# Rotary tables of three supertiles in one set, and the sums of one group's second V weights declared a step later

## The chip, the cores and the metric

The kernel runs on one core of a Trainium2 chip. The metric is the device time of one execution in microseconds; of several runs the median is taken.

## What is computed

A two-layer encoder over 2048 tokens of width 1024. In each layer a normed row is projected to eight sections; four feed a softmax attention over the token's own chunk of 64 and the eight before it (8 heads of 64, a learned bias by distance), four feed a retention (4 heads of 128) whose queries and keys are turned by rotary phases. Both outputs are gated, put side by side and projected back onto the row.

```
def rotary_tables(positions, dim):
    ang = positions.astype(jnp.float32)[:, None] * inv_freq[None, :]
    return jnp.cos(ang), jnp.sin(ang)
...
    hn = rms_norm(x, norm_gain)
    proj = hn @ w_in.astype(hn.dtype)
    aq, ak, av, ag, rq, rk, rv, rg = jnp.split(proj, cuts, axis=-1)
    ya = chunked_rel_attention(aq, ak, av, rel_bias)
    yr = chunkwise_retention(rq, rk, rv, cos, sin)
    y = jnp.concatenate([ya * jax.nn.silu(ag), yr * jax.nn.silu(rg)], axis=-1)
    return x + y @ w_out.astype(x.dtype)
```

## The kernel before

The tokens are cut into 4 supertiles `n` of 512 (16 token tiles of 128), the heads of a layer into 4 groups `s`. For each group and supertile two dense products are made, `dense_T` (tiles `dT`, line 778: q and k of both parts, tokens along the columns) and `dense_V` (tiles `dV`, line 797: v, the retention's v and the gates), each of four 512-wide tiles of 24 matmuls; operands are split in a high and a low half (`hTh`, `hTl` for the rows, `whT`, `wlT`, `whV`, `wlV` for the weights), three products for each pair. In between stand the attention and retention of the supertile before.

`run()` sets the order. In each round it advances the dense generator by eight matmuls, ticks the list of postponed steps (`later(k, ...)` runs a step k rounds on), takes one step of the attention, and draws steps from a background list `bg`: as many as the declared steps still to come, divided by the rounds left, rounded up. The engines' order is the program's order; only the queue of SyncE (SP), which issues nearly all DMAs, is ordered by the scheduler after the start. Sums and retention products share four small PSUM buffers in rotation, the dense tiles two.

Four pieces matter here. `tables(ns, wk)` works out cosine and sine for the supertiles `ns` in four workspaces: DMAs of the positions (line 90), an angle on ScalarE (100), a reduction of 15 steps on VectorE (lines 94, 97, 98, 107, 114, 116), sine activations on ScalarE behind a load of their function table (118, 119, 121), and stores to DRAM (127 to 130). Workspaces are 256 columns wide for each supertile, on 128 partitions. `norms_from_input(ts, ...)` norms the token tiles `ts` of the first layer: load of x (line 1239), square on ScalarE (212), root on GpSimd (POOL, 219), scaling on VectorE (1251), high and low half (234, 238), and two DMA transposes (243, 244) into `hTh`, `hTl`. `prep_V(l, s, g)` quantizes the next group's V weights in four sections: load (305), square with its sum along the row (320), a cast (327), a sum over partitions by a one-column matmul `msV` (334), a scale (336 and 151 to 155), and the two halves (341 on ScalarE, 344 on VectorE). `rest(k)` in it lets k background steps pass between a square and its sum. The attention's softmax is at lines 845 to 857 (scores, scale and maximum, exponential, product with the bias on POOL, transpose `pT`), its output at 865 to 877, the retention's products `r` at 899, the rotary turn on POOL at 719 to 721, and the evacuations of the dense tiles at 677 to 697 (`qq`, `kk`) and 805 to 815 (`v`, `rv`, `gt`).

The first group's start is an order written out by hand, in which `u` is a step of the table generator `t1` for supertiles 1 and 2. The tables of supertile 3 ride in the second `norms_from_input`, a step per round, on two halves of the same buffers.

Of the kernel before, what the change touches and what calls it, by code (L numbers as in the profile page):

```python
# [10 lines left out]
F32 = mybir.dt.float32  # L11
# [7 lines left out]
P = 128  # L19
# [8 lines left out]
def hybrid_trunk(ctx: ExitStack, tc: tile.TileContext, x, pos, gain, gcol, w_in, w_out, rel, fgain,  # L28
                 invf, dmask, dcol, out):
    nc = tc.nc  # L30
    SEQ, D = x.shape
# [14 lines left out]
    w4 = ctx.enter_context(tc.tile_pool(name="w4", bufs=3))  # L46
# [36 lines left out]
    def tables(ns, wk):  # L83

        ang, k, r, k2 = wk
        pi = k2.bitcast(I32)
        for i, n in enumerate(ns):
            for hf in range(2):
                o = n * 512 + hf * 256
                sp.dma_start(pi[hf * 64:(hf + 1) * 64, i * 256:(i + 1) * 256], pos[None, o:o + 256].to_broadcast([64, 256]))  # L90
        yield

        def mulsub(dst, kk, c):
            dve.scalar_tensor_tensor(out=dst, in0=kk, scalar=-c, in1=dst, op0=ALU.mult, op1=ALU.add)

        def rnd(dst, src, mul):
            dve.tensor_scalar(dst, src, mul, MAGIC, op0=ALU.mult, op1=ALU.add)
            dve.tensor_scalar(dst, dst, -MAGIC, None, op0=ALU.add)

        act.activation(ang, pi, AF.Copy, scale=invf_sb[:, 0:1])  # L100
        yield
        rnd(k, ang, 1.0 / P1)
        yield
        for c in (PA, PB, PC):
            mulsub(ang, k, c)
            yield
        dve.scalar_tensor_tensor(out=k2, in0=k, scalar=-(PD + PE_), in1=ang, op0=ALU.mult, op1=ALU.add)
        yield
        rnd(k2, k2, 1.0 / TWO_PI)
        yield  # L110
        for kk, c in ((k2, QA), (k, PD), (k2, QB), (k, PE_), (k2, QC)):
            mulsub(ang, kk, c)
            yield
        dve.tensor_scalar(ang, ang, PI_CL, -PI_CL, op0=ALU.min, op1=ALU.max)
        yield
        dve.scalar_tensor_tensor(out=k, in0=ang, scalar=-1.0, in1=ang, op0=ALU.mult, op1=ALU.max)
        yield
        act.activation(r, ang, AF.Sin)
        act.activation(k2, k, AF.Sin, scale=-1.0, bias=quarter[:, 0:1])
        yield  # L120
        act.activation(ang, r, AF.Copy, scale=-1.0)
        yield
        def store(i, n, hf):
            sl = slice(hf * 64, hf * 64 + 64)
            cs = slice(hf * 256, hf * 256 + 256)
            ws = slice(i * 256, i * 256 + 256)
            sp.dma_start(tab_d[n][0, 0:64, cs], k2[sl, ws])
            sp.dma_start(tab_d[n][0, 64:128, cs], k2[sl, ws])
            sp.dma_start(tab_d[n][1, 0:64, cs], ang[sl, ws])
            sp.dma_start(tab_d[n][1, 64:128, cs], r[sl, ws])  # L130
            if hf == 1:
                tab_done.add(n)

        for hf in range(2):
            store(0, ns[0], hf)
            if len(ns) > 1:
                later(7 + 4 * hf, lambda hf=hf: store(1, ns[1], hf))
        yield

    TAB_STEPS = 18  # L140
# [301 lines left out]
    def prep_V(l, s, g):  # L442
        nm = f"V{l}_{s}"
        g.vh = b3.tile([P, KT, 512], F16, tag="wh", name=f"wh{nm}")
        g.vl = b3.tile([P, KT, 512], F16, tag="wl", name=f"wl{nm}")
        c0 = s * P
        sts = []

        def ld(j):
            o = VSEC[j] * 512 + c0  # L450
            sts.append(load_sec(w_in[l, :, o:o + P], f"{nm}{j}"))

        def sq(j):
            return sumsq(sts[j], f"{nm}{j}", g.vh[:, :, j * P:(j + 1) * P])

        def cv(j, s_):
            return convert(sts[j], g.vh[:, :, j * P:(j + 1) * P], g.vl[:, :, j * P:(j + 1) * P], s_)

        def rest(k):
            for _ in range(k):  # L460
                yield

        ld(0)
        ld(1)
        yield
        iv = [None] * 3
        m1 = [None] * 2
        for j in range(2):
            yield
            m1[j] = lowp(sq(j), f"{nm}{j}")  # L470
            yield from rest(3)
            m = allsum(m1[j], f"{nm}{j}")
            sv, iv[j] = norm_scale(m, f"{nm}{j}", gains[l].i)
            yield from cv(j, sv)
            ld(2 + j)
        yield from rest(1)
        m2 = sq(2)
        yield
        yield from rest(1)
        m3 = sq(3)  # L480
        dve.tensor_tensor(m2, m2, m3, op=ALU.add)
        m2 = lowp(m2, f"{nm}2")
        yield
        yield from rest(2)
        m = allsum(m2, f"{nm}2")
        sv, iv[2] = norm_scale(m, f"{nm}2", gains[l].i)
        for _ in V_units(l, s, g, iv, nm):
            pass
        yield from cv(2, sv)
        yield from cv(3, sv)  # L490
        g.vdone = 4
# [145 lines left out]
    def later(k, fn):  # L637
        deferred.append([k, fn])
# [556 lines left out]
    def push(gen, steps):  # L1195
        bg.append([gen, steps])
# [17 lines left out]
    def grp(l, s):  # L1214
        if (l, s) not in groups:
            groups[l, s] = Grp()
        return groups[l, s]
# [12 lines left out]
                pull(min(-(-todo // max(left, 1)), todo))  # L1230
            left -= 1

    def norms_from_input(ts, spaces, rows, tab):

        def load(k):
            u = us[k]
            u.x = spaces[k] if spaces else w4.tile([P, D], F32, tag="w4", name=f"xin{u.t}")
            if not spaces:
                sp.dma_start(u.x, x[u.t * P:(u.t + 1) * P, :])

        def sq(k):
            u = us[k]
            u.h = [h_[:, :, u.t % 4 * P:(u.t % 4 + 1) * P] for h_ in hT_of(0, u.t // 4)]
            u.ss = squares(u.x.rearrange("p (k c) -> p k c", c=P), u.nm, u.h[0])

        def root(k):
            us[k].rs = rms_of(us[k].ss, gains[0].m, gains[0].e, us[k].nm)

        def mul(k):
            u = us[k]  # L1250
            dve.scalar_tensor_tensor(out=u.x, in0=u.x, scalar=u.rs[:, 0:1], in1=gains[0].b, op0=ALU.mult, op1=ALU.mult)

        def hi(k):
            us[k].rows = rows[k % 2]
            rows_hi(us[k].rows, us[k].x)

        def lo(k):
            rows_lo(us[k].rows, us[k].x)

        def dma(k):  # L1260
            transpose_rows(us[k].rows, *us[k].h)

        us = []
        for t in ts:
            u = St()
            u.t, u.nm = t, f"n0_{t}"
            us.append(u)
        plan = {0: [lambda: load(0)]}
        add = lambda r, fn, k: plan.setdefault(r, []).append(lambda: fn(k))
        for k in range(4):  # L1270
            if k:
                add(4 * k - 4, load, k)
            for i, fn in enumerate((sq, root, mul, hi, lo, dma)):
                add(3 + 4 * k + i, fn, k)
        for r in range(21):
            for fn in plan.get(r, ()):
                fn()
            next(tab, None)
            yield
        for _ in tab:  # L1280
            yield

    xa = b3.tile([P, 2, D], F32, tag="wh", name="xa")
    xb = b3.tile([P, 2, D], F32, tag="wl", name="xb")
    xs0 = [xa[:, 0, :], xa[:, 1, :], xb[:, 0, :], xb[:, 1, :]]
# [48 lines left out]
    late = [h_.rearrange("p k c -> p (k c)").bitcast(F32)[:, i * D:(i + 1) * D] for f in far for h_ in f for i in range(2)]  # L1334
# [70 lines left out]
            vu.append(V_units(0, 0, g00, scs["V0"].i + scs["V2"].i, "V0_0"))  # L1405
        next(vu[0])

    t1 = tables((1, 2), [xs0[1 + i // 2][:, i % 2 * 512:(i % 2 + 1) * 512] for i in range(4)])
    x8 = (sp.dma_start(late[t - 8], x[t * P:(t + 1) * P, :]) for t in range(8, 12))
    steps = {"x8": lambda: go_on(x8), "d": lambda: go_on(d0), "t": lambda: go_on(t0), "u": lambda: go_on(t1), "r": lambda: go_on(rl_), "g": lambda: go_on(gs),  # L1410
             "Tu": T_un, "Vu": V_un, "bs": lambda: go_on(bs0), "bt": lambda: go_on(bt0)}
# [26 lines left out]
    for l in range(DEPTH):  # L1438
        gO = [Grp(), Grp()]
        go = Grp()  # L1440
        for s in range(NSW):
            g = grp(l, s)
            for n in range(NS):
                first = (l, s, n) == (0, 0, 0)
# [11 lines left out]
                if (l, s) == (0, 0) and 0 < n < NS - 1:  # L1456
                    if n == 1:
                        push(t1, TAB_STEPS - 7)
                    pairs = [xs0[0], w4.tile([P, D], F32, tag="w4", name="rows8") if n == 1 else xs0[1]]
                    pairs = [(w_[:, 0:D], w_[:, D:2 * D]) for w_ in (r_.bitcast(F16) for r_ in pairs)]  # L1460
                    push(norms_from_input(range(4 * n + 4, 4 * n + 8), late[0:4] if n == 1 else None, pairs,
                                          iter(()) if n == 1 else tables((3,), [xs0[3][:, i * 256:(i + 1) * 256] for i in range(4)])), 21)
                if (l, s, n) == (0, 1, 1):
                    for l_ in range(1, DEPTH):
                        gr = gain_scale(l_)
# [17 lines left out]
                    run(dT, att, 12 if last else 10 if n == 0 else 18 if (l, s, n) == (0, 0, NS - 1) else 22 if (l, s) == (0, 0) else 24)  # L1483
                if n == NS - 1:
                    if s + 1 < NSW:
                        push(prep_V(l, s + 1, grp(l, s + 1)), 23)
                    else:
                        push(with_turn(prep_O(l, 1, gO[1], go), us), 12)
                run(dense_V(l, s, n, g, st), att, 24 if n == NS - 1 and s < NSW - 1 else 12)
# [90 lines left out]
```

## Time and profile before

| | |
|---|---|
| runs | 2061.4, 2063.08, 2059.04 us; median 2061.4 |
| profiled execution | 2062.49 us, span 2060.7 us |
| mean granted clock of TensorE | 0.995 |
| busy, share of span | PE 97%, VectorE 60%, ScalarE 55%, POOL 33% |

The span is the time from the first to the last instruction in the profiled execution. PE is TensorE's matmuls, PEld its weight loads, DVE VectorE, ACT ScalarE, POOL GpSimd, SP SyncE. A row of the timeline gives start (us), duration (us), engine, line, operation, what it writes and reads, and in brackets how long the engine stood idle before it and what released it. Rows grouped by line give the busy time in all, the mean in ns, and the idle time before.

### The profile page before, as it was taken

Reading aid. Unit: us, or ns where it says so; the run is one execution under the profiler, and the core shown is the slowest. Engines: PE = TensorE matmul, PEld = TensorE weight load, DVE = VectorE, ACT = ScalarE, POOL = GpSimd, SP = SyncE. Lnnn points to the kernel's source line nnn. Section 1 sums busy time; section 2 is a strip of 40 time slices with the busy share of each in tenths; the row PEclk is TensorE's granted clock in tenths of the full one; section 3 lists DMA queues with packets and bytes.
Section 4 is the critical chain, followed back from the end, with each engine's and each line's share of the span. In section 5 each row is a group of like instructions: output and inputs, shape, how many; then the busy total and the mean of one; then the engine's idle time right before and its main releaser. Section 6 shows DMA issues by size and latency. Waiting matters only on the chain. (4 is left out here: it accounts for less than half of the span.)

```text
span 2060.7 us, 39339 instructions
## 1 busy us (share of the span) xinstructions
PE 1999.4 (97%) x14038; PEld 1052.9 (51%) x14038; DVE 1228.1 (60%) x3804; ACT 1134.8 (55%) x2526; POOL 688.1 (33%) x701
## 2 busy tenths in 40 slices
PE   6988999999999999999999999999999999999998
PEld 4444555555555555554444555555555555555544
DVE  6776666565556555666553556555655566557643
ACT  6556665556565645555444546655656565455432
POOL 0344343434334434430003443444333334333100
PEclk9999999999999999999999999999999999999999
DMA  8778664547584754899774546554746775658864
GB/s 227 169 161 178 155 148 109 112 114 164 117 185 113 165 128 101 174 209 263 219 185 113 124 104 156 116 126 103 158 117 150 148 155 124 129 115 187 224 203 139
DMA packets 645701, 313.64 MB, mean 152 GB/s; under 512 B 459232, under 2 KB 602080, under 8 KB 645504
## 3 DMA queue, kind: packets, MB, share of 16 engines
q1 hardware_dynamic: 645504, 311.12, 65.6%
q8 instruction: 110, 1.80, 0.4%
q14 instruction: 87, 0.71, 0.1%
HBM read 123.26 MB, written 41.98 MB: 80 GB/s over the span
## 5 line engine op out<-in xcount | busy, mean ns | idle before, releaser
L855 POOL TENSOR_TENSOR pq<-sc,pq 128x640 f16<-128x640 f32 (+4 forms) x256 | 319.4, 1248 | 860.5 <-ACT pq L854 443.8
L852 ACT ACTIVATE sc<-sc,mq,cT 128x640 f32<-128x640 f32 (+4 forms) x256 | 218.4, 853 | 615.6 <-DVE rl L871 309.7
L797 PE MATMUL dV<-whV,hTh 128*128 128x512 f16 x1024 | 353.9, 381 | 7.3 <-DVE gt L815 6.1
L797 PE MATMUL dV<-whV,hTl 128*128 128x512 f16 x1024 | 353.8, 381 | 0.0
L797 PE MATMUL dV<-wlV,hTh 128*128 128x512 f16 x1024 | 353.8, 381 | 0.0
L778 PE MATMUL dT<-hTh,whT 128*128 128x512 f16 x1008 | 346.6, 379 | 2.7 <-DVE kk L697 1.3
L778 PE MATMUL dT<-hTl,whT 128*128 128x512 f16 x1008 | 346.6, 379 | 0.0
L778 PE MATMUL dT<-hTh,wlT 128*128 128x512 f16 x1008 | 346.6, 379 | 0.0
L797 PEld LDWEIGHTS <-hTh 128*128 128x128 f16 x2048 | 197.0, 98 | 224.7 <-DVE gt L815 10.0
L778 PEld LDWEIGHTS <-whT 128*128 128x128 f16 x2016 | 192.1, 98 | 207.7 <-issue 1.6
L849 DVE CUSTOM_DVE_ANT_0 sc<-S,bias 128x640 f32<-128x640 f32 (+4 forms) x256 | 188.3, 735 | 88.8 <-PE S L846 87.4
L1172 PE MATMUL dO<-whO,yly 128*128 128x512 f16 x504 | 191.0, 379 | 1.7 <-DMA yly<-hTl 1.1
L1172 PE MATMUL dO<-whO,yhy 128*128 128x512 f16 x504 | 191.0, 379 | 1.0 <-DMA yhy<-hTh 1.0
L1172 PE MATMUL dO<-wlO,yhy 128*128 128x512 f16 x504 | 191.0, 379 | 0.0
L854 ACT ACTIVATE pq<-sc 128x640 f16<-128x640 f32 (+4 forms) x256 | 171.5, 670 | 8.1
L797 PEld LDWEIGHTS <-hTl 128*128 128x128 f16 x1024 | 99.4, 98 | 112.4 <-issue 3.9
L1172 PEld LDWEIGHTS <-yhy 128*128 128x128 f16 x1008 | 98.1, 98 | 113.7 <-DMA yhy<-hTh 1.5
L778 PEld LDWEIGHTS <-wlT 128*128 128x128 f16 x1008 | 97.2, 98 | 113.7 <-issue 6.0
L845 PE MATMUL S<-k,q 128*128 128x128 f16 (+3 forms) x592 | 142.4, 267 | 0.0
L865 PE MATMUL o<-v,pT 128*128 128x65 f16 x1120 | 129.8, 193 | 6.4 <-DMA pT<-pq 5.5
L866 PE MATMUL o<-v,pT 128*128 128x64 f16 x1120 | 130.1, 195 | 0.0
L846 PE MATMUL S<-k,q 128*128 128x128 f16 (+3 forms) x592 | 129.7, 267 | 0.0
(359 smaller groups left out, 3476.5 us busy)
## 6 DMA issues: line engine op xcount, KB each, us to landing
q<-qq SPq DMA_DIRECT2D x128, 128.0 KB, 2.4
yyy<-y_d SPq DMA_DIRECT2D x32, 512.0 KB, 4.5
stT<-in_w_in_dram SPq DMA_DIRECT2D x27, 512.0 KB, 4.8
stV<-in_w_in_dram SPq DMA_DIRECT2D x26, 512.0 KB, 4.6
k<-kk SPq DMA_DIRECT2D x128, 64.0 KB, 2.0
swp<-rot SPq DMA_DIRECT2D x64, 128.0 KB, 3.1
tabc<-tab SPq DMA_DIRECT2D x32, 256.0 KB, 3.0
tabs<-tab SPq DMA_DIRECT2D x32, 256.0 KB, 3.1
```

The source lines that it names most:

```text
L778: pe.matmul(ps, w_[:, j, kt, :], h_[:, kt, :], start=(m == 0), stop=(m == 23))
L797: pe.matmul(ps, h_[:, kt, a * P:(a + 1) * P], w_[:, kt, :], start=(m == 0), stop=(m == 23))
L845: pe.matmul(o, st.q[:, hx, 0, cs], k_, start=True, stop=False)
L846: pe.matmul(o, st.q[:, hx, 1, cs], k_, start=False, stop=True)
L849: dve.tensor_tensor_reduce(out=v, in0=S[:, 0:w], in1=g.bias[hx][:, 640 - w:640], scale=1.0, scalar=-3.0e38, op0=ALU.add, op1=ALU.max, accu ...
L852: act.activation(v, v, AF.Exp, bias=m[:, 0:1], scale=g.c[:, 0:1])
L854: act.activation(pq[:, 0:w], v, AF.Copy)
L855: pool.tensor_tensor(pq[:, w:2 * w], v, pq[:, 0:w], op=ALU.subtract)
L865: pe.matmul(o[:, 0:65], u.p[:, b, :], v_[:, 0:65], start=(b == 0), stop=False)
L866: pe.matmul(o[:, 0:64], u.p[:, b, :], v_[:, 65:129], start=False, stop=False)
L1172: pe.matmul(ps, h_[:, kt, :], w_[:, kt, :], start=(m == 0), stop=(m == 23))
```

## The change

The tables of supertiles 1, 2 and 3 are worked out together, 768 columns wide, by the generator that made those of 1 and 2; a further buffer `wkc` serves as fourth workspace. `norms_from_input` loses its tables. The stores of the two later supertiles are postponed by 3, 6, 9 and 12 rounds instead of 7 and 11 for one. For the second group of the first layer, `prep_V` rests a step more between the first, second and last square and their sums, and its declared number of steps is 26 instead of 23.

```diff
-            if len(ns) > 1:
-                later(7 + 4 * hf, lambda hf=hf: store(1, ns[1], hf))
+            for i in range(1, len(ns)):
+                later(6 * i - 3 + 3 * hf, lambda i=i, hf=hf: store(i, ns[i], hf))
...
+        first = (l, s) == (0, 1)
...
-            yield from rest(3)
+            yield from rest(3 + first)
...
-        yield from rest(2)
+        yield from rest(2 + first)
...
-    def norms_from_input(ts, spaces, rows, tab):
+    def norms_from_input(ts, spaces, rows):
...
-            next(tab, None)
-            yield
-        for _ in tab:
             yield
...
-    t1 = tables((1, 2), [xs0[1 + i // 2][:, i % 2 * 512:(i % 2 + 1) * 512] for i in range(4)])
+    wk = [xb.rearrange("p a c -> p (a c)")[:, 0:768], xs0[1][:, 0:768], xb.rearrange("p a c -> p (a c)")[:, 768:1536],
+          w4.tile([P, D], F32, tag="w4", name="wkc")[:, 0:768]]
+    t1 = tables((1, 2, 3), wk)
...
-                                          iter(()) if n == 1 else tables((3,), [xs0[3][:, i * 256:(i + 1) * 256] for i in range(4)])), 21)
+                    push(norms_from_input(range(4 * n + 4, 4 * n + 8), late[0:4] if n == 1 else None, pairs), 21)
...
-                        push(prep_V(l, s + 1, grp(l, s + 1)), 23)
+                        push(prep_V(l, s + 1, grp(l, s + 1)), 26 if (l, s) == (0, 0) else 23)
```

How instructions move is seen in the order of each engine. (From line 463 on, the changed file counts one line more, up to the end of `norms_from_input`.) On ScalarE, at the end of the second `norms_from_input`, before:

```order
L854 ACTIVATE pq_0_1_2_1_2142<-sc_0_1_2_1_2137 128x640
L212 ACTIVATE hTh_3_150,ssn_15_2147<-xin_1903 128x8x128
L118 ACT_TABLE_LOAD
L118 ACTIVATE xb<-xb 128x256
L119 ACTIVATE xb<-xb,quarter 128x256
L730 ACTIVATE rot_0_2_2_1889<-rot_0_2_2_1889 128x512
L947 ACTIVATE state_0_0_1229<-state_0_0_1229 128x128
L121 ACTIVATE xb<-xb 128x256
L805 ACTIVATE v_0_2_2000<-dV_0_2_1_2102 128x2x64
L806 ACT_TABLE_LOAD
L806 ACTIVATE gt_0_2_1_2185<-dV_0_2_1_2102,ughV_0_735 128x256
L807 ACTIVATE rv_0_2_1_2184<-dV_0_2_1_2102,urvV_0_733 128x128
```

And after, at the same place:

```order
L855 ACTIVATE pq_0_1_2_1_2135<-sc_0_1_2_1_2130 128x640
L212 ACTIVATE hTh_3_150,ssn_15_2140<-xin_1903 128x8x128
L731 ACTIVATE rot_0_2_2_1889<-rot_0_2_2_1889 128x512
L948 ACTIVATE state_0_0_1236<-state_0_0_1236 128x128
L806 ACTIVATE v_0_2_1996<-dV_0_2_1_2095 128x2x64
L807 ACTIVATE gt_0_2_1_2175<-dV_0_2_1_2095,ughV_0_738 128x256
L808 ACTIVATE rv_0_2_1_2174<-dV_0_2_1_2095,urvV_0_736 128x128
```

The three table activations and two loads of function tables are gone from between token tile 15's square (`ssn_15`) and the evacuation of a dense tile. (In the names of the dense tiles the first number is the group, the second the supertile.)

On TensorE, at the first sum of the second group's V weights (`msV_10`) in the dense tile `dV_0_3_2`, whose first third stands ahead of the attention step that ends with `r_0_11`. Before:

```order
L899 LDWEIGHTS rot_0_2_3_1980
L899 MATMUL r_0_11_3064<-rot_0_2_2_1889,rot_0_2_3_1980 128x128
L334 LDWEIGHTS ones
L334 MATMUL msV_10_3069<-mbV_10_2971,ones 128x1
L797 LDWEIGHTS hTh_3_150
L797 MATMUL dV_0_3_2_3022<-wlV_0_199,hTh_3_150 128x512
L797 LDWEIGHTS hTh_3_150
L797 MATMUL dV_0_3_2_3022<-whV_0_198,hTh_3_150 128x512
```

After, where `dV_0_3_2` begins:

```order
L900 MATMUL r_0_10_2992<-rv_0_2_2_2272,kt_0_2_2361 128x128
L334 LDWEIGHTS ones
L334 MATMUL msV_10_3004<-mbV_10_2953,ones 128x1
L798 LDWEIGHTS hTh_3_150
L798 MATMUL dV_0_3_2_3016<-whV_0_198,hTh_3_150 128x512
L798 LDWEIGHTS hTl_3_151
L798 MATMUL dV_0_3_2_3016<-whV_0_198,hTl_3_151 128x512
```

The sum has moved ahead of the tile's first eight matmuls and of the attention step behind them. The square that feeds it has kept its place on ScalarE; before:

```order
L852 ACTIVATE sc_0_2_2_1_2960<-sc_0_2_2_1_2960,mq_0_2_2_1_2961,cT_0_676 128x640
L854 ACTIVATE pq_0_2_2_1_2965<-sc_0_2_2_1_2960 128x640
L320 ACTIVATE whV_1_2919,m1V_10_2969<-stV_10_2921 128x8x128
L730 ACTIVATE rot_0_3_2_2678<-rot_0_3_2_2678 128x512
L947 ACTIVATE state_0_0_1229<-state_0_0_1229 128x128
```

After:

```order
L853 ACTIVATE sc_0_2_2_1_2942<-sc_0_2_2_1_2942,mq_0_2_2_1_2943,cT_0_679 128x640
L855 ACTIVATE pq_0_2_2_1_2947<-sc_0_2_2_1_2942 128x640
L320 ACTIVATE whV_1_2901,m1V_10_2951<-stV_10_2903 128x8x128
L731 ACTIVATE rot_0_3_2_2660<-rot_0_3_2_2660 128x512
L948 ACTIVATE state_0_0_1236<-state_0_0_1236 128x128
```

The second sum (`msV_11`) moves in the same way, ahead of the first eight matmuls of `dT_1_0_0`; its square moves ahead of one softmax step. The third sum keeps its place on TensorE, and one of its two squares moves ahead of a softmax step.

More of the change, by code (lines that the diff above doesn't have):

```diff
@@ L1460, in hybrid_trunk @@
                     pairs = [(w_[:, 0:D], w_[:, D:2 * D]) for w_ in (r_.bitcast(F16) for r_ in pairs)]
-                    push(norms_from_input(range(4 * n + 4, 4 * n + 8), late[0:4] if n == 1 else None, pairs,
-                                          iter(()) if n == 1 else tables((3,), [xs0[3][:, i * 256:(i + 1) * 256] for i in range(4)])), 21)
+                    push(norms_from_input(range(4 * n + 4, 4 * n + 8), late[0:4] if n == 1 else None, pairs), 21)
                 if (l, s, n) == (0, 1, 1):
```

## The prediction

> **What bounds the kernel now.** I read the page first, then the waits of TensorE, then cuts of the 3.41 us that its clock moves in, and last the timeline at the three places that the change touches. The page says which engine sets the time:
>
> ```profile
> span 2060.7 us, 39339 instructions
> PE 1999.4 (97%) x14038; PEld 1052.9 (51%) x14038; DVE 1228.1 (60%) x3804; ACT 1134.8 (55%) x2526; POOL 688.1 (33%) x701
> ```
>
> TensorE (PE) works for 97% of the span. The change takes no matmul away, so it can gain or lose only where PE stands still or runs slow. Between 60 and 300 us, which holds all that is edited, the waits of PE are these (us in total, times, longest):
>
> ```profile
> PE dV L797 <- DVE gt L815: 4.9, 2, 3.3
> ...
> PE msV L334 <- DVE ya L877: 3.4, 3, 1.5
> ...
> PE dT L778 <- DVE kk L697: 1.3, 1, 1.3
> ...
> PE dT L778 <- DMA hTh<-xa: 0.8, 1, 0.8
> PE dT L778 <- DVE qq L680: 0.6, 1, 0.6
> ```
>
> The first row holds the stall beside the tables of supertile 3, the second the sums of the V weights, the third and the fifth stand in the tables of supertiles 1 and 2. The second price of a stall is the clock. In cuts of 3.41 us, each row gives the stretch, PE's busy time, and behind POOL's the granted clock:
>
> ```profile
> 90.32:93.73 3.41, 2.23 (x14) 1.16 (x14) 1.96 (x8) 1.81 (x3) 0.00 (x0) 1.00 0.44 104
> 117.62:121.03 3.41, 0.78 (x6) 0.28 (x5) 3.41 (x4) 2.81 (x11) 3.33 (x3) 1.00 0.61 125
> 121.03:124.44 3.41, 3.24 (x13) 1.64 (x14) 2.99 (x10) 0.65 (x1) 1.94 (x3) 0.50 0.98 305
> 179.05:182.47 3.42, 1.21 (x6) 0.36 (x4) 0.00 (x0) 3.40 (x8) 2.82 (x3) 1.00 0.83 204
> 182.47:185.88 3.41, 2.36 (x6) 0.89 (x7) 3.26 (x9) 0.39 (x2) 0.00 (x0) 0.50 0.67 187
> 185.88:189.30 3.42, 3.42 (x26) 2.08 (x25) 1.38 (x5) 3.33 (x6) 1.40 (x1) 0.50 0.43 153
> ```
>
> A stretch with 0.78 or 1.21 us of work is followed by one at half clock; a stretch with 2.23 is not. A stretch at half clock and 2.36 us busy is followed by a second. So I price a wait of over some 2.2 us within one stretch at 3.41 / 2 = 1.7 us more, if PE is what is late just after. Whether a wait falls into one stretch or over two is chance.
>
> **A, tables of 768 columns (70 to 91.5 us).** Sizes and slack:
>
> ```profile
> L116 DVE SCALAR_TENSOR_TENSOR xa<-xa 128x512 f32<-128x512 f32 x1 | 0.7, 693 | 0.0
> ...
> L116 DVE SCALAR_TENSOR_TENSOR xb<-xb 128x256 f32<-128x256 f32 x1 | 0.4, 419 | 0.0
> L114 DVE TENSOR_SCALAR xa<-xa 128x512 f32<-128x512 f32 x1 | 0.4, 417 | 0.0
> ...
> L114 DVE TENSOR_SCALAR xb<-xb 128x256 f32<-128x256 f32 x1 | 0.3, 285 | 0.0
> ```
>
> ```profile
> L119 ACT ACTIVATE xb<-xa,quarter 128x512 f32<-128x512 f32 x1 | 0.7, 705 | 0.0
> ...
> L119 ACT ACTIVATE xb<-xb,quarter 128x256 f32<-128x256 f32 x1 | 0.5, 492 | 0.0
> ```
>
> ```profile
> 74.16 0.29 DVE L811 SCALAR_TENSOR_TENSOR v<-dV,v 128x128 f16<-128x128 f32 x1 [0.64 <-ACT rv L807]
> ...
> 82.41 0.69 DVE L727 TENSOR_TENSOR rot<-raw,rot 128x512 f16<-128x512 f32 x1 [0.64 <-POOL pq L855]
> ...
> 83.82 0.69 DVE L680 SCALAR_TENSOR_TENSOR qq<-dT,qq 128x512 f16<-128x512 f32 x1 [0.71 <-ACT qq L677]
> ...
> 87.18 1.28 ACT L118 ACT_TABLE_LOAD   x1
> ...
> 91.50 0.38 PE L778 MATMUL dT<-hTh,whT 128*128 128x512 f16 x1 [1.28 <-DVE kk L697]
> ```
>
> Another 256 columns cost 0.27 us in a SCALAR_TENSOR_TENSOR, 0.13 in a TENSOR_SCALAR, 0.21 on ScalarE (ACT). Ahead of the table load at 87.18 DVE has nine steps of the first kind and four of the second: 9 x 0.27 + 4 x 0.13 = 3.0 us more, against slack of 0.64 + 0.64 + 0.71 = 2.0. So the softmax step ahead of that load, and the load, come 1.0 later; the three ACTIVATEs behind it add 3 x 0.21 = 0.64; kk L694 and L697 stand behind them in order, and PE at 91.50 behind L697. That is **+1.6**, between 0.6 (only the ACTIVATEs count) and 2.6 (1.0 of the slack isn't there, since POOL's work beside stretches some of these steps). The waits of 0.6 and 1.3 become some 1.0 and 2.5 us. That is enough for a half clock where it falls into one stretch: 0.6 x 1.7 = **+1.0**.
>
> Here the Trainium skill speaks against me: "TensorE: Matmul & The Clock Gate", section "HAM oscillation — how this bites in real kernels", has as its rule no idle gaps over about 3.4 us, so that this wait would cost its own length alone and the sum would be 1.0 lower. The stretch at 121.03 disagrees: it runs at 0.50 behind one that had 0.78 us of work, not none.
>
> **D, the queue of SyncE (118 to 133 us).** The eight stores for two supertiles instead of four for one now stand among these transfers, and the two first loads of x for supertile 3 come right ahead of the transposes of token tile 11. The transpose that now stands right behind the loads, the second of tile 11, which stands clear of them, and PE's first use of tile 11:
>
> ```profile
> L243 SPq DMA_TRANSPOSE hTh<-xa x1: 2434/2434/2434, 121.9 to 121.9; - x1
> ...
> DMA to landing us min/median/max: 5.2/5.2/5.2
> ```
>
> ```profile
> L244 SPq DMA_TRANSPOSE hTl<-rows x1: 1231/1231/1231, 129.8 to 129.8; - x1
> ...
> DMA to landing us min/median/max: 3.0/3.0/3.0
> ```
>
> ```profile
> 133.02 1.46 PE L778 MATMUL dT<-hTh,whT 128*128 128x512 f16 x6
> ```
>
> The second half of tile 11 is issued at 129.8 and lands at 132.8; PE needs it in its third matmul, 133.4 (six matmuls in 1.46 us start 0.22 apart). With 5.2 it would land at 135.0. The loads have been under way some 4 us by then, so I take the middle: **+0.7**, between 0 and 1.5. The loads of positions move too, to the queue near 45 us, where the next transposes wait for ACT anyway: 0.
>
> **B, tables of supertile 3 gone (158 to 194 us).** Fifteen DVE steps, four ACTIVATEs and two table loads leave, and eight stores behind them.
>
> ```profile
> 173.51 0.23 PE L899 MATMUL r<-rv,dT 128*128 128x128 f16 x1 [1.29 <-DVE dT L907]
> ...
> 181.40 0.55 POOL L219 TENSOR_TENSOR rsn<-ssn,mhalf 128x1 f32<-128x1 f32 x1
> ...
> 183.38 1.28 DVE L1251 SCALAR_TENSOR_TENSOR xin<-xin,rsn,gb 128x1024 f32<-128x1024 f32 x1
> ...
> 183.52 0.61 PE L797 MATMUL dV<-whV,hTh 128*128 128x512 f16 x1 [3.26 <-DVE gt L815]
> ...
> 193.93 1.25 PE L778 MATMUL dT<-hTh,whT 128*128 128x512 f16 x5 [0.77 <-DMA hTh<-xa]
> ```
>
> The waits at 173.51 and 183.52 lose their cause. But what is late next is the norm of token tile 15: POOL takes its root (181.40) behind the rotary turn, DVE scales the row (183.38), then softmax, the high half, POOL, SyncE's transpose, and PE at 193.93. POOL keeps its work and its order; it comes 1.29 earlier with PE. The scaling then starts at 181.40 + 0.55 - 1.29 = 180.7 instead of 183.38, and with the same chain behind it PE is released **-2.7** us at 193.93. The ends are -1.4 (POOL no earlier) and -4.8, by this row:
>
> ```profile
> L94 DVE SCALAR_TENSOR_TENSOR xb<-xb 128x256 f32<-128x256 f32 x8 | 6.7, 843 | 0.0
> ```
>
> Eight steps of the tables take 843 ns instead of the 419 of the row above, beside POOL; if all of these 8 x 0.42 = 3.4 us came to POOL's chain, it would be -1.4 - 3.4. PE is then early for the new release at 191.2: from 183.52 to 193.93 it takes 10.41 - 0.77 - 2.89 (half of 2.36 + 3.42, at half clock) = 6.75 us, and it starts at 183.52 - 3.26 - 1.29 = 178.97, so it idles 191.2 - 185.7 = 5.5 us in several pieces; for the stretch behind the start that is 0.5 x 1.7 = **+0.8**.
>
> **C, the sums of the second V weights (234 to 268 us).** By the order in the section on the change, the first sum comes a round earlier, not later: the total of declared steps rises, and two steps are drawn per round for longer. Its square stays where it is.
>
> ```profile
> 234.69 0.38 PE L797 MATMUL dV<-whV,hTh 128*128 128x512 f16 x1
> ...
> 237.02 1.04 ACT L320 ACTIVATE whV<-stV 128x1024 f16<-128x1024 f32 x1
> ...
> 238.19 0.16 DVE L327 CAST mbV<-m1V 128x1 bf16<-128x1 f32 x1 [2.79 <-ACT whV L320]
> ...
> 238.98 0.16 PE L334 MATMUL msV<-mbV,ones 128*128 128x1 bf16 x1 [1.22 <-DVE ya L877]
> ```
>
> PE reaches the sum at 234.69 and must hold it until the cast has ended, 238.40: 3.7 us, with a third of a dense tile and an attention step queued behind that could have run. Their work, 238.98 - 1.22 - 234.69 = 3.07, follows: they end at 241.47 instead of 239.01, +2.4. The other two waits of the row of 3.4 go, as their squares come earlier: -(3.4 - 1.2) = -2.2. Together **+0.2**, between -1.5 (casts earlier than now, by slack that I don't see) and +1.5 (the third wait stays). A single wait of 3.7 nearly always empties one stretch: 0.9 x 1.7 = **+1.5**.
>
> **Sum.** 1.6 + 1.0 + 0.7 - 2.7 + 0.8 + 0.2 + 1.5 = +3.1 on the profiled execution's 2062.49. That one stands 1.1 above the median of the runs, 2061.4; so 2064.5.
>
> **Rivals.** *Each wait earns its half clock, and C two stretches,* as at 182.47 to 189.30: 1.6 + 1.7 + 0.7 - 2.7 + 1.7 + 0.2 + 3.4 = +6.6, 2068.0, slower. For it: every wait over 2.2 us within one stretch that the rows show. Against: none is sure to fall so. It decides once two of the three do. Chance 0.25.
> *The norm of tile 15 doesn't bind:* then 1.29 + 3.26 + 0.77 of waits and 2.89 of half clock go, -8.2 in place of -1.9, and the sum is -3.2: 2058.2, or 2057 if A keeps its clock. For it: the wait at 193.93 is only 0.77 long. Against: the scaling can't start before POOL's root. Chance 0.13.
> *No half clock for waits under 3.4 us,* by the mechanism that a stretch must be empty: without 1.0 and 0.8 the sum is +1.3, 2062.7. The row at 121.03 speaks against it. This is the page's rule above. Chance 0.07.
> *The edit does what its words say,* each sum behind its square: 1.6 + 1.0 + 0.7 - 1.9 - 3.4 = -2.0, 2059.4. Only if the printed order weren't what runs. Chance 0.05. My forecast has 0.5.
>
> About 0.2%, 4.1 us, is what a measurement of this kernel can tell from no change. Slower by more (over 2065.5): 0.22 of the first rival and 0.21 of the forecast, whose own 8 in 10 are 2061 to 2068: 0.43. Faster (under 2057.3): half of the second rival, some of the fourth and the tail: 0.15. Within: 0.42. The range from 2058.0 to 2069.5 takes in the first rival and the second in part.
>
> **What would show it.** In the profile after: kk L697 releases PE 1.3 to 2 us later against the first tables' start, with a wait of about 2.5; the waits for gt L815 lose the one of 3.3 us, and dT L778 waits for hTh of tile 15 for longer than 0.8; msV L334 waits once, some 3.7 us, for its own cast, with a half-clock stretch behind it. I am wrong if PE no longer waits at supertile 3's start, if msV's first wait is short, or if the clock stays at 1.00 behind waits of 2.5 us.

## The result and the profile after

The change makes the kernel slower: 2068.05 us against 2062.02 us (medians of 21 runs each), a ratio of 1.0028 with a 95% interval of 1.0021 to 1.0034, or 4.3 to 7.0 us. The profiled execution after takes 2068.73 us with a span of 2066.5.

The waits of TensorE between 60 and 300 us, after (us in total, times, longest):

```profile
PE msV L334 <- DVE mbV L327: 3.5, 1, 3.5
PE o L866 <- DMA pT<-pq: 2.8, 3, 1.1
...
PE dT L779 <- DVE kk L698: 2.2, 1, 2.2
PE dT L779 <- DMA hTh<-rows: 1.2, 1, 1.2
PE dT L779 <- DVE qq L681: 1.2, 1, 1.2
PE dT L779 <- DMA hTh<-xa: 0.8, 1, 0.8
```

The 4.9 us behind gt L815 are gone, and so are the three waits of a sum for an evacuation. (Of the 4.9, 3.3 stood beside the tables of supertile 3. The other 1.6 stood near 68 us, ahead of the steps that change; this execution is 1.6 us late there, by a stretch at half clock from 44.86 us, and that wait takes it up.) In their place stand one wait of 3.5 us of the first sum for its own cast, longer waits in the first tables (kk and qq, and 1.0 us in two for rot), and waits for DMA transposes (pT, hTh<-rows). The granted clock in cuts of 3.41 us (the column behind POOL's) around the wait for sh L908, which before has too, behind supertile 3's start, and around the first sum:

```profile
119.96:123.37 3.41, 1.10 (x15) 0.48 (x12) 3.04 (x2) 3.38 (x12) 3.41 (x3) 1.00 0.70 136
123.37:126.78 3.41, 2.69 (x12) 1.33 (x12) 2.98 (x11) 0.26 (x1) 2.69 (x4) 0.50 0.46 109
126.78:130.20 3.42, 3.42 (x10) 1.22 (x9) 2.81 (x8) 3.11 (x5) 1.16 (x1) 0.50 0.70 148
...
191.64:195.05 3.41, 1.32 (x10) 0.52 (x9) 3.41 (x10) 1.73 (x8) 0.55 (x2) 1.00 0.64 138
195.05:198.46 3.41, 2.59 (x9) 1.02 (x10) 1.38 (x6) 2.45 (x6) 0.71 (x1) 0.50 0.81 162
198.46:201.88 3.42, 3.42 (x25) 1.97 (x24) 1.08 (x4) 0.51 (x2) 0.68 (x1) 0.50 1.50 241
...
239.42:242.84 3.42, 0.40 (x4) 0.28 (x5) 1.06 (x4) 2.26 (x3) 0.53 (x1) 1.00 0.62 173
242.84:246.25 3.41, 2.73 (x8) 1.04 (x8) 2.01 (x12) 2.33 (x9) 3.33 (x4) 0.50 0.43 99
246.25:249.66 3.41, 3.41 (x36) 2.02 (x34) 2.16 (x6) 1.75 (x2) 1.27 (x1) 1.00 0.06 17
```

Each stretch at full clock with 1.32 us of work or less is followed by one at half clock, as before. A halved stretch with 2.59 or 2.69 us of work had a second behind it, one with 2.73 had none.

Where the time went, by the start of the same matmul in both traces: PE is 3.2 us late when kk releases it (94.66 against 91.50), 5.8 late at the first matmul of supertile 2 (138.83 against 133.02), 2.5 at the first of supertile 3 (196.43 against 193.93). The two halved stretches behind that take most of this gain back: just ahead of the first sum PE is 5.1 late (239.57 against 234.46). It is 8.8 late behind the first sum (243.54 against 234.69), and 6.2 behind the third (273.90 against 267.68); it ends 5.8 later. So in this execution the tables' part makes 5.1 us and the sums some 1.1.

### The profile page after: what moved, and what is told of

It reads as the page before. It is cut to its first block, busy times and chain, and to the rows that moved or that the text cites. A ratio compares the mean times of both kernels' runs of the same rounds, so it can differ in the third digit from the quotient of the medians.

```text
span 2066.5 us, 39310 instructions
## 1 busy us (share of the span) xinstructions
PE 2002.7 (97%) x14038; PEld 1052.8 (51%) x14038; DVE 1222.8 (59%) x3789; ACT 1133.0 (55%) x2520; POOL 686.1 (33%) x701
```

## The experiments

Each is compared with before in runs on one chip, 9 to 11 runs of it against 21 to 33 of before; a ratio of 1.0010 is 2.1 us.

**The two parts alone.** The tables' part has the whole diff but that of `prep_V` and its declared steps; the sums' part has only these.

> The tables' part of the change alone. From the two traces, theory 1 says that this part carries the loss: PE comes to 91.5 of before some 3.2 us late (first tables wider and SyncE's queue longer ahead of them), loses some 3 us more to transposes that land late around 120 to 148, and gets back about 3 us and two half-clock stretches where the tables of supertile 3 were, of which a later half clock takes most: about +4.5 us against before (+3 to +6). Theory 2, that the loss is the sum which PE holds for 3.5 us, says that the tables alone are within 1.5 us of before.

> The V sums' part alone (rests one step longer, 26 declared steps). Theory 1: one wait of 3.5 us and about one half-clock stretch come, waits of 1.2, 0.7 and 1.5 us go: +1 us against before (-0.5 to +2.5). Theory 2, that this wait and the clock behind it carry the loss: +3.5 to +5 us.

The tables alone: 1.0017 (1.0008 to 1.0026), +3.5 us. The sums alone: 1.0013 (1.0004 to 1.0022), +2.7 us. The sum of the two, 6.2, is about the whole change's 5.8: the loss is shared. Theory 2 falls for the tables, which cost more than the 1.5 us it gave them. Theory 1's range holds the tables; the sums lie 0.2 above its range, but their own interval (0.8 to 4.5) reaches into it. The profile of the sums alone shows how they can cost more than its +1: PE is 0.3 late ahead of the first sum and 2.8 behind the third, with this clock:

```profile
234.08:237.49 3.41, 0.74 (x10) 0.45 (x9) 1.62 (x7) 1.69 (x3) 0.00 (x0) 1.00 0.55 150
237.49:240.91 3.42, 2.17 (x7) 0.80 (x7) 1.55 (x8) 2.81 (x8) 3.38 (x3) 0.50 0.35 84
240.91:244.32 3.41, 3.41 (x28) 2.25 (x27) 0.85 (x7) 1.15 (x1) 1.75 (x2) 0.50 0.23 55
```

In this execution the wait of 3.5 us fell so that two stretches ran at half clock; in that of the whole change it was one.

**The rests without the declared steps.**

```diff
-            yield from rest(3)
+            yield from rest(3 + (((1, 1))[j] if first else 0))
...
-        yield from rest(2)
+        yield from rest(2 + (1 if first else 0))
```

> The rests one step longer, but the declared steps left at 23, so that by the order each sum stands a round behind its place of before. Theory 1 (the place of the sum against its square is all): the three waits of 3.4 us in all before a sum go, and nothing takes their place: -3.4 us against before (-4.5 to -1.5). Rival: the queue of the evacuations behind the squares is what is late, and PE waits for it an instruction later: 0 (-1 to +1).

It took 1.0026 (1.0016 to 1.0036), +5.4 us. The waits ahead of the sums did go, but a larger one came, in TensorE's waits from 225 to 320 us:

```profile
PE dV L798 <- ACT whV L341: 7.3, 1, 7.3
```

The steps that the rests push back end with the weights' high half (L341). With 23 declared steps it is written 7.3 us after the next group's dense V tile wants to begin. Both expectations missed that. The three more declared steps buy this deadline (with them, in the sums alone, no such wait stands there), and pay by drawing the first sum a round ahead.

**What the first tables' width costs.** Both kernels start from the tables alone, so the sums are as before. In the first, supertile 3 isn't worked out and gets the columns of supertile 2.

```diff
-    t1 = tables((1, 2, 3), wk)
+    t1 = tables((1, 2), [w_[:, 0:512] for w_ in wk])
...
-            for i in range(1, len(ns)):
-                later(6 * i - 3 + 3 * hf, lambda i=i, hf=hf: store(i, ns[i], hf))
+            for i, n in ((1, 2), (2, 3)) if len(ns) > 1 else ():
+                later(6 * i - 3 + 3 * hf, lambda n=n, hf=hf: store(1, n, hf))
```

> The tables' part with 512 columns as before: supertile 3 isn't worked out, its stores take the columns of supertile 2, and its positions aren't loaded, so that the wide steps and the longer queue of positions are gone while the stores and the loads of x stay where the change puts them. Theory 1: the 3.2 us at the first tables go, so about +1 us against before (-1.5 to +2.5) with kk L698 releasing PE near 91.5 as before, and the late transposes of 120 to 148 still there. Rival: the widths cost nothing that PE sees, and the stores in the queue are the cost: +4 us as with the full tables.

In the second kernel, the positions of supertile 3 are loaded by a step `pl` of the rounds behind the start.

```diff
+        places(every[:2])
+        late_pos.append(lambda: places(every[2:]))
...
+"pl": lambda: late_pos[-1](),
...
-"xdma4 xhi5 xmul6 bt",
+"xdma4 xhi5 xmul6 bt pl",
```

> The tables' part alone, with the two loads of supertile 3's positions issued some rounds later, behind the first supertile's table reads in SyncE's queue. If the longer queue near 46 us makes POOL's second turn and what follows late (theory 1b), PE is released by kk L697 about 0.8 us earlier than with the tables' part alone: +2.5 us against before instead of +3.5. If only the widths count (rival), the same +3.5 as the tables' part alone.

With 512 columns: 1.0006 (0.9997 to 1.0015), +1.2 us, as theory 1 said. Against the tables' 3.5 that puts width and positions together at some 2.3 us, but the two intervals overlap, so the times alone don't show it. With the positions later: 1.0015 (1.0006 to 1.0023), +3.1 us, which doesn't tell +2.5 from +3.5. The waits between 80 and 97 us say more. With 512 columns:

```profile
PE dT L778 <- DVE kk L697: 1.3, 1, 1.3
```

With 768 columns and the positions later:

```profile
PE dT L784 <- DVE kk L703: 2.2, 1, 2.2
PE r L905 <- DVE rot L733: 0.5, 1, 0.5
```

The wait for kk stays at 2.2 without the longer queue of positions and returns to 1.3 with 512 columns: it is the width. Between 80 us and kk's release PE loses 2.4 to 3.2 us against before in each of the five profiles with 768 columns, and at most 0.7 in each of the six others. The positions are less clear. Where they come later, the wait for rot is 0.5 instead of the 1.1 of the tables alone, and the loss 2.4 instead of 3.2, as theory 1b says; but the last two kernels of this section lose 2.4 as well, with all positions loaded together.

**What the queue of SyncE costs.** Before, with the stores of supertile 2 issued at the four new rounds, each half's twice:

```diff
-            if len(ns) > 1:
-                later(7 + 4 * hf, lambda hf=hf: store(1, ns[1], hf))
+            for i in (1, 2) if len(ns) > 1 else ():
+                later(6 * i - 3 + 3 * hf, lambda hf=hf: store(1, ns[1], hf))
```

> Before, with the stores of supertile 2 issued at the new rounds 3 and 6, and once more at 9 and 12 (the same data again, in place of supertile 3's stores): only SyncE's queue is as after the change; tables, widths and sums are as before. Theory 1 (the loads of x pushed right ahead of token tile 11's transposes): PE waits 1 us or more for hTh at the start of supertile 2 near 134 us, and for pT near there; +2 us against before (+0.5 to +3.5). Rival (the wide steps alone carry the tables' loss): the wait at 134 us is absent or is made up by the wait at 183 us, 0 (-0.7 to +0.7).

It took 1.0018 (1.0009 to 1.0026), +3.7 us (1.9 to 5.4): the place of the stores and of the loads of x behind them costs about as much as the whole tables' part. Between 110 and 150 us, TensorE waits there for

```profile
PE r L899 <- DVE sh L907: 2.1, 1, 2.1
PE o L865 <- DMA pT<-pq: 1.7, 2, 1.0
PE r L899 <- ACT dT L903: 1.3, 1, 1.3
PE dT L778 <- DMA hTh<-rows: 0.9, 1, 0.9
```

and in before for

```profile
PE r L899 <- DVE sh L907: 2.1, 1, 2.1
PE r L899 <- ACT dT L903: 0.6, 1, 0.6
PE r L899 <- DVE dT L907: 0.2, 1, 0.2
```

Two waits for pT and one for token tile 11's rows are new, 2.6 us in all; from 122 to 150 us PE goes from 0.4 early to 2.2 late. In the profile of the sums alone, which leaves this queue as it was, there is a wait for pT too:

```profile
PE o L866 <- DMA pT<-pq: 1.9, 1, 1.9
```

So the 1.7 for pT isn't shown to be the queue's. The wait for token tile 11's rows is: no profile with the stores at their old place has it, and each with the stores moved does, 0.9 us here, 1.2 after, 3.9 with the tables alone and 3.7 with 512 columns. The profile shows 2.6 us, which the interval holds; whether more falls elsewhere stays open.

**What the tables taken away are worth.** Before, with supertile 3 taking over the tables of supertile 2:

```diff
+    def taken_over():
+        tab_d[3] = tab_d[2]
+        tab_done.add(3)
+        yield
...
-                                          iter(()) if n == 1 else tables((3,), [xs0[3][:, i * 256:(i + 1) * 256] for i in range(4)])), 21)
+                                          iter(()) if n == 1 else taken_over()), 21)
```

> Before, with the tables of supertile 3 neither worked out nor stored (supertile 3 takes those of supertile 2): what the change takes away, without what it pays elsewhere. Theory 1 (the norm of token tile 15 binds next): the waits at 173.5 and 183.5 go, PE comes to the first matmul of supertile 3 some 2.7 us earlier and waits there for hTh; -2 us against before (-3.5 to -0.5), the rest lost to a half clock behind that wait. Rival (nothing binds next): all 5.3 us of waits and the half clock there go, -5 to -8 us.

It took 0.9986 (0.9977 to 0.9995), -2.9 us, as theory 1 said. Between 165 and 195 us TensorE now waits for

```profile
PE o L865 <- DMA pT<-pq: 1.1, 1, 1.1
PE r L899 <- DVE dT L907: 1.1, 1, 1.1
PE dT L778 <- DMA hTh<-xa: 1.0, 1, 1.0
PE r L899 <- ACT dT L903: 0.6, 1, 0.6
```

In before there were 3.3 for gt, 1.3 for dT and 0.8 for hTh in this stretch, 5.4 in all; now it is 3.8, of which 1.0 for hTh<-xa, the rows of token tile 15. The first matmul of supertile 3 starts at 190.80 against 193.93, and the stretch from 191.37 runs at half clock.

**A version that beats both.** The rests are chosen so that each sum comes when its square has ended and the weights keep their deadline:

```diff
-            yield from rest(3)
+            yield from rest(3 + (2 if first and j == 0 else 0))
...
-        yield from rest(2)
+        yield from rest(2 + first)
...
-                        push(prep_V(l, s + 1, grp(l, s + 1)), 23)
+                        push(prep_V(l, s + 1, grp(l, s + 1)), 26 if (l, s) == (0, 0) else 23)
```

> Before, with 26 declared steps as in the change, but the first rest two steps longer, the second as before, the last one longer: by the order the first sum keeps its place of before, and the other two stand as after the change. Theory 1 (a sum costs by its place against its square and against the evacuations behind it): the first wait of 1.2 us stays, the other two (2.2 us) go, no wait of 3.5 us and no half clock come: -2 us against before (-3 to -0.5). Rival (drawing two steps a round is itself the loss, by more work for ACT and VectorE in each round): 0 to +3 us, as with the sums' part alone.

It took 0.9988 (0.9979 to 0.9997), -2.5 us, as theory 1 said: faster than before, by little, and than the change. Among TensorE's waits from 230 to 275 us:

```profile
PE msV L334 <- DVE ya L878: 1.2, 1, 1.2
```

Of the sums only the first waits, and no stretch there runs at half clock.

**The tables with an easier queue, alone and with those sums.** The scratch workspace takes the rotating buffer, the stored cosine takes `xs0[1]`, and supertile 3's stores are declared later. A row of token tile 13 is written over that workspace before half of supertile 3's cosines are stored, so these two kernels turn that half by wrong angles; they serve for the time alone.

```diff
-                later(6 * i - 3 + 3 * hf, lambda i=i, hf=hf: store(i, ns[i], hf))
+                later(7 + 4 * hf if i == 1 else 28 + 3 * hf, lambda i=i, hf=hf: store(i, ns[i], hf))
...
-    wk = [xb.rearrange("p a c -> p (a c)")[:, 0:768], xs0[1][:, 0:768], xb.rearrange("p a c -> p (a c)")[:, 768:1536],
-          w4.tile([P, D], F32, tag="w4", name="wkc")[:, 0:768]]
+    wk = [xb.rearrange("p a c -> p (a c)")[:, 0:768], w4.tile([P, D], F32, tag="w4", name="wkc")[:, 0:768], xb.rearrange("p a c -> p (a c)")[:, 768:1536],
+          xs0[1][:, 0:768]]
```

> The tables' part alone, with the scratch workspace in the buffer that the loads of x rotate through and the stores of supertile 3 declared 28 and 31 rounds on: by the order the loads of x stand 12 places earlier in SyncE's queue, as in before, and half of supertile 3's stores stand behind token tile 11's transposes. Theory 1 (the place of the loads and stores is +3.7, the wide steps +2.3, the tables gone -2.9): about 0 against before (-1.5 to +1.5), with no wait of 1 us or more for hTh at the start of supertile 2. Rival (the tables' part loses by its width alone): +3.5 us, as before this edit.

> The last kernel's tables with the V sums of the kernel in which the first rest is two steps longer and the last one longer. Theory 1, if the parts add: 0 - 2.5 = -2.5 us against before (-4.5 to -0.5). Rival (the two parts meet, so that a wait taken away at one is paid at the other): 0 (-1 to +1).

Alone it took 1.0009 (1.0001 to 1.0018), +1.9 us, between the two expectations. With the sums it took 1.0002 (0.9992 to 1.0012), +0.4 (-1.6 to +2.5), where -2.5 had been expected. The parts as measured, +1.9 and -2.5, add to -0.6, which lies in that interval, so nothing here shows that they meet. Theory 1's own sign failed: between 110 and 150 us the wait for token tile 11 is there, and longer.

```profile
PE dT L778 <- DMA hTh<-rows: 2.8, 1, 2.8
```

The queue of SyncE in that trace shows that the edit took the loads out of the way, but not the stores:

```profile
127.41 0.63 SPq L128 DMA_DIRECT2D tab<-xa  x1
...
130.64 0.46 SPq L130 DMA_DIRECT2D tab<-xb  x1
131.21 1.25 SPq L857 DMA_TRANSPOSE pT<-pq  x1
132.56 1.26 SPq L243 DMA_TRANSPOSE hTh<-rows  x1
```

ScalarE has written tile 11's high half (L234) by 128.54, 1.6 us later than before, and its transpose is issued at 132.56, 4.7 us later than before's 127.86. So 1.6 us come from what stands ahead of this norm, the wide first tables among it, and the larger part from the six stores that fill SyncE's queue from 127.41 on, five of tables and one of a result, with pT behind them. A kernel with these stores out of the way as well wasn't run.

## Why the prediction was right, and where it was off

It had slower with 0.43, hardly above the 0.42 for a time within 0.2%, and 2064.5 in a range from 2058.0 to 2069.5; 2068.05 lies in it. That this falls on the first rival's 2068.0 is luck: of its three half clocks, the one behind kk didn't come in the profile after, the sums had one stretch, not two, and B's came, but over two stretches, while a term that it priced as the forecast did, D, was the worst miss. The mechanisms held, the sizes less so. By the runs of the parts the terms are 2.3 (A), 3.7 (D), -2.9 (B) and 2.7 (C), against 2.6, 0.7, -1.9 and 1.7; they add to the 5.8 measured, but each has an interval of 4 us or more, so that the sum agrees better than it had to.

**A, the width.** The step is right: nine and four wider steps of VectorE come ahead of the table load, ScalarE's three wider ACTIVATEs behind it, and kk L698 ends late. Between 80 us and kk's release PE loses 3.1 us, not 1.6, above the range given. The table load comes at 89.70 instead of 87.18, 2.5 us later where the forecast had 1.0, and the ACTIVATEs behind it add 0.65, as forecast. VectorE, after:

```profile
76.29 1.91 DVE L107 SCALAR_TENSOR_TENSOR wkc<-xa,xb 128x768 f32<-128x768 f32 x1
...
78.57 1.17 DVE L97 TENSOR_SCALAR wkc<-wkc 128x768 f32<-128x768 f32 x1
79.78 1.50 DVE L98 TENSOR_SCALAR wkc<-wkc 128x768 f32<-128x768 f32 x1
...
85.80 0.69 DVE L681 SCALAR_TENSOR_TENSOR qq<-dT,qq 128x512 f16<-128x512 f32 x1 [0.71 <-ACT qq L678]
```

POOL beside it:

```profile
75.42 1.97 POOL L720 TENSOR_TENSOR raw<-raw,tabc 128x512 f32<-128x512 f32 x1 [11.36 <-DMA swp<-raw]
77.34 1.99 POOL L721 TENSOR_TENSOR swp<-swp,tabs 128x512 f32<-128x512 f32 x1
79.41 1.46 POOL L722 TENSOR_TENSOR raw<-raw,swp 128x512 f32<-128x512 f32 x1
```

The wide steps are priced nearly right. Alone they take 0.96 and 0.55; beside POOL's turn one SCALAR_TENSOR_TENSOR took 1.91 and the two TENSOR_SCALARs 1.17 and 1.50, but the steps of before were stretched there too (1.64, 1.04 and 1.10 us instead of 0.69, 0.43 and 0.69). All thirteen take 3.5 us more than before, against 3.0 forecast, and they start 0.3 later behind the wider angle on ScalarE (L100), which no term had. What was mis-sized is the slack: of the 2.0 us taken off, 1.2 gave way (the range's upper end of 2.6 had 1.0 give way, and neither the stretching nor the angle). The 0.71 us ahead of qq are still there in full, since ScalarE's qq, for which VectorE waits, is itself 2.0 us later (85.17 against 83.19). In ScalarE's order it follows a step that waits for POOL to be through with its turn (L617, 81.60 against 79.72). That turn starts 1.2 us later, its first two steps took 1.97 and 1.99, where before had 1.27 and 1.71, and it ends 2.0 us later, and with it rot and the softmax behind it. That also gave the waits for rot that no term had.

The halved stretch from 44.86 us has no part in this: PE is 0.1 us late at 80 us. (The profiles of the stores alone and of the better version, whose tables are as before, have one near 44 us too.) The half clock expected behind kk didn't come in this execution, by a hair: 2.0 of the 2.2 us of wait fell into the stretch from 92.65, which had 1.40 us of work. With the tables alone the stretch there had 1.21, and the next ran at 0.50.

```profile
92.65:96.06 3.41, 1.40 (x7) 0.68 (x7) 1.96 (x8) 1.82 (x4) 0.00 (x0) 1.00 0.40 91
96.06:99.48 3.42, 2.63 (x18) 1.27 (x15) 0.43 (x2) 3.38 (x7) 0.75 (x2) 1.00 0.40 91
```

**D, the queue.** The mechanism was named, the size was the worst miss: 0.7, between 0 and 1.5, against +3.7 by itself. The term priced only the second half of tile 11 with one longer landing. In the trace after, the loads hold up the issue of the transposes too:

```profile
130.62 1.05 SPq L1240 DMA_DIRECT2D xin<-in_x_dram  x2
131.77 0.38 SPq L959 DMA_DIRECT2D y_d<-yr  x1
132.25 1.24 SPq L858 DMA_TRANSPOSE pT<-pq  x1
133.58 3.07 SPq L243 DMA_TRANSPOSE hTh<-rows  x1
136.75 1.26 SPq L244 DMA_TRANSPOSE hTl<-rows  x1
```

The first half's issue takes 3.07 us, and 2.60 in the run that moves the stores alone, where the loads stand ahead of it too; it takes 1.26 in before and with the easier queue, where they don't. It lands 5.2 us behind its issue instead of 3.1, and the second half waits behind it. It is also issued 5.7 us later than before (133.58 against 127.86), where the high half that it carries is written only 3.2 later; the term had no price for that. And pT, which goes the same way, was left out.

**B, the tables gone.** Right in mechanism: -2.7 and 0.8 for the clock were forecast, -1.9 in all; the tables gone by themselves give -2.9 (-4.7 to -1.0), which holds the forecast. Its reason is in the trace after:

```profile
185.32 0.55 POOL L219 TENSOR_TENSOR rsn<-ssn,mhalf 128x1 f32<-128x1 f32 x1
...
185.91 1.28 DVE L1252 SCALAR_TENSOR_TENSOR xin<-xin,rsn,gb 128x1024 f32<-128x1024 f32 x1 [2.36 <-POOL rsn L219]
```

VectorE now stands idle for the root of tile 15, and scales the row as it comes. The rival that nothing binds next falls. One sign was off: PE waits 0.8 us for tile 15's rows after, as before, not longer, and 1.0 with the tables gone by themselves. The clock's price was 0.8, a half of one stretch; with the tables gone by themselves it was one stretch, in the whole change two.

**C, the sums.** The reading of the order held: the first sum comes a round early and PE waits for its cast, 3.54 us (3.7 forecast), and the other two waits go. The term with its clock was 1.7; by itself the part costs 2.7 (0.8 to 4.5), which holds it. In the two profiles it is 2.4, with two halved stretches, and 1.1, with one. The rival by which the edit does what its words say falls, and the run of the rests alone shows that even then the time would not have come out lower: another deadline stands behind them.

**The clock.** The rival by the rule of the Trainium skill ("TensorE: Matmul & The Clock Gate", section "HAM oscillation — how this bites in real kernels"), no loss below about 3.4 us of idle time, falls: in the trace after, the stretch from 119.96 had 1.10 us of work, in several pieces, and the next two ran at 0.50. The forecast's own boundary, a wait of over some 2.2 us within one stretch, came near: the last section puts it at 2.0.

## What to carry to other kernels

A step that is made later in a paced list can come out earlier, where its declared length rises with it and sets the pace; read the place of the instruction, and then the deadline of what stands last in the list. A DMA that is moved costs what it delays in its queue, and the first to ask about is the transpose that TensorE waits for next, with its issue time and its landing. Idle time in a chain is slack only if what ends it doesn't come later too; of 2.0 us taken off here, 0.8 wasn't. When work is taken from a busy stage, price the gain by the chain that is late next, here 2.9 us of 5.3 us of waits.

## What the runs showed of the hardware

In the profiles of all twelve kernels, from 60 to 2040 us, the granted clock of a stretch of 3.41 us goes by TensorE's work (its busy time in the profile) in the one before. The 36 stretches at full clock that were followed by one at half clock had 1.40 us of work or less, and the only other one with so little is that from 92.65 above. The boundary is narrow: this one, of the run that moves the stores alone, shows the same 1.40:

```profile
927.58:930.99 3.41, 1.40 (x21) 0.73 (x19) 1.86 (x5) 3.38 (x5) 1.40 (x1) 1.00 1.13 301
930.99:934.40 3.41, 3.41 (x10) 1.19 (x9) 3.01 (x7) 2.29 (x6) 0.25 (x1) 0.50 1.39 291
```

So some 2.0 us of idle time within one such stretch, in one piece or several, cost a half clock here. A halved stretch was followed by a second in all 12 cases with 2.69 us of work or less, and in none with 3.02 or more; of two between, 2.73 had none and 2.78 had one. So an idle time of 3.5 us cost one or two such stretches, by where it fell.
